# The output projection's block products: weight sums formed in DRAM ahead of time, operand sums stored raw, and a hand-written order

## The chip, the cores and the metric

One Trainium2 chip, one of its cores. The metric is the device time of one launch in microseconds. The kernel before was run three times: 2400.41, 2401.74 and 2396.83 us, median 2400.41. A separate profiled launch took 2404.39 us, of which 2402.6 us lie between its first and its last instruction; the trace and all its views are of that launch.

## What is computed

One layer of a streaming encoder, on 512 prompt frames and 32 frames of a running stream, 544 columns together, with a model width of 2048. The part that matters here:

```python
h = layer_norm(x, ln_in_g, ln_in_b)
proj = h @ w_in                       # 2048 -> 4928
o_h = hgrn2(...)                      # 8 heads of 128, gated, normalised
o_a = mla_attention(...)              # 8 heads of 128
mix = concat([o_h, o_a]) @ w_out      # 2048 -> 2048: the output projection
h1  = layer_norm(ALPHA * h + mix, ln1_g, ln1_b)
ff  = conv_ffn(h1)                    # 2048 -> 5632 -> 2048
y   = layer_norm(ALPHA * h1 + ff, ln2_g, ln2_b)
```

All data are float32. A product in that precision is made of three passes over rounded parts: a value x is split into h = round(x) and l = x - h, and w*a becomes wh*ah + wh*al + wl*ah.

## The kernel before

Features lie on the 128 partitions and the 544 frames along the free axis, in two halves of 272 (`NI`). One matmul multiplies a 128x128 weight tile by 128x272 activations. Weights arrive as 128x1024 float32 tiles of 512 KB (`raw`). ScalarE rounds each to `wh` and VectorE subtracts to get `wl`.

**Stages.** First come the input norm and projections, then attention (`proj_pair` and `attend`, woven together up to about 300 us), then the heads of the recurrence (about 300 to 727 us): for each head h, `divided_qf` and `divided_ig` multiply on TensorE, while `levels(h)` and `finish(h)` of the heads before are stepped in between. After that comes the output projection (about 727 to 963 us), then the feed-forward network to the end.

**Seven products for eight.** Where a product is "divided", a 2x2 block product of weights and activations is done as seven block products (11, s1, s2, s4, s3, 12, 22), with sums of weight blocks and sums of activation blocks as operands. The heads' input products, the feed-forward ones, and groups 1 to 4 of the output projection are of this kind. One such block product is 8 x 3 = 24 matmuls into one PSUM bank.

**Where the sums come from, for the output projection.** The activation sums s1, s2, s3, s4 are made in `finish(h)`. Its tail, in 18 steps, forms each sum with VectorE in `ab`, rounds it with ScalarE (`high`, L988), subtracts with VectorE (`low`, L991), and stores the pair by one DMA from tile `hl`, which has two buffers, to `ou_dr` (L992, `ous` in the trace). The tail therefore needs four ScalarE copies, four VectorE subtractions and four stores per head. The weight sums are made in place while the products run: `Blocks.plus` (L1257) adds two raw tiles on VectorE, and `plus_dma` (L1260) adds another block from DRAM by an accumulating DMA on GpSimd's queue.

**The output projection itself.** `out_first` multiplies group 0 (tiles 0 and 1 of 16) with 192 matmuls, both halves, while the last head's `finish` is stepped. The residual h0 is then loaded into `za` and `zb` (`zt[k]`, L1401; k < 8 on GpSimd's queue, the others on SyncE's), the stored sums into `su` (L1407, GpSimd's queue). `Norm.first` for each half adds tiles 0 and 1 (L1124), gets the column mean through TensorE (L1113, L1118) and centres both. Groups 5 and 6 follow, first half only, with `gemm_half`, 96 matmuls each. All this is ordered by the planner of the tile framework, which places an instruction of a part without a written order as soon as its engine and its inputs are free by its own reckoning.

A block with a written order (`tc.manual_schedule`) then plays groups 1 to 4. The list `oitems` has 11 and 12 of each group first (8 products), then s1, s2, s4, s3, 22 of each group (20 products). `play` does for item n: the sink of item n-1 (`out_sink`, L1734 or L1737, VectorE adds the PSUM bank into `zt`), the matmuls (L1704), the preparation of the weights of item n+2 (L1246, L1247) and the forming for item n+3 (L1257). Products 11, s2, s3 and 22 of a group share one bank; 12, s1 and s4 use the other kind. The sinks of s4 and 22 also call `close_rows` (L1725), which centres two tiles and adds them and their squares to the norm's sums (GpSimd, ScalarE, L1154). The second halves of eight `cH`/`cL` tiles hold s3 during this time; GpSimd puts it there (`place_s3`, L1774), after L1062 has saved the original, and SyncE brings that back at the end (`place_a21`, L1779). Group 7 and the second halves of groups 5 and 6 follow (913 to 963 us).

Of the kernel before, what the change touches and what calls it, by code (L numbers as in the profile page):

```python
# [15 lines left out]
P = 128  # L16
D = 2048
KD = D // P
# [41 lines left out]
def tile_encoder_step(ctx, tc, xp, xs, w_in, w_in4, w_kr, w_q_b, w_kv_b, w_out, w_out4, w_up, w_gate, w_down, w_down2,  # L60
# [17 lines left out]
    ou_dr = {n: [dram.tile([P, 2, 4, NI], F32, name=f"ou{n}{i}", tag=f"ou{n}{i}") for i in range(2)]  # L78
             for n in ("s1", "s2", "s3", "s4")}
    a21_dr = [dram.tile([P, 2, NI], F32, name=f"a21d{k}", tag=f"a21d{k}") for k in range(HK)]  # L80
# [93 lines left out]
    def weave(fills, chains, ratio):  # L174
        chain = (s for g in chains for s in g)
        credit = 0.0
        for g in fills:
            for _ in g:
                credit += ratio
# [201 lines left out]
    with tc.tile_pool(name="mp", bufs=1) as mp, tc.tile_pool(name="psa", bufs=4, space=PSUM) as psa:  # L381
# [273 lines left out]
        run(proj_pair(0))  # L655
        weave([proj_pair(1)], [attend(0)], 2.0)
        weave([proj_pair(2)], [attend(1)], 2.0)
        weave([proj_pair(3)], [attend(2)], 2.0)
        weave([head_ig(0)], [attend(3)], 2.0)
# [15 lines left out]
    with tc.tile_pool(name="gp", bufs=1) as gp, tc.tile_pool(name="psg", bufs=1, space=PSUM) as psg:  # L675
# [60 lines left out]
        class Divided:  # L736
# [174 lines left out]
        def finish(h):  # L911
# [4 lines left out]
            dma(ab[:, 1], d3_dr[h // 2][:, h % 2])  # L916
            vT = gp.tile([P, 5, P], F32, name="vT", tag="vT", bufs=1)
# [66 lines left out]
            hl = {}  # L984

            def high(name, x):
                hl[name] = gp.tile([P, 2, NI], R, name="hl", tag="hl", bufs=2)
                A.activation(hl[name][:, 0], x, AF.Copy)  # L988

            def low(name, x):  # L990
                V.tensor_tensor(out=hl[name][:, 1], in0=x, in1=hl[name][:, 0].bitcast(F32), op=ALU.subtract)  # L991
                dma(ou_dr[name][h // 4][:, :, h % 4], hl[name].bitcast(F32))  # L992
# [6 lines left out]
            high("s1", ab[:, 0])  # L999
            opposite(ab[:, 1], ab[:, 1], o[:, NI:])  # L1000
            yield
            low("s1", ab[:, 0])
            high("s2", ab[:, 1])
            yield
            low("s2", ab[:, 1])
            opposite(ab[:, 1], ab[:, 1], o[:, :NI])
            high("s4", ab[:, 1])
            yield
            low("s4", ab[:, 1])
# [18 lines left out]
        with tc.manual_schedule(engines=MANUAL):  # L1028
# [7 lines left out]
            beside_from(0, finish(1), range(18))  # L1036
            for h in range(2, HEADS):
                s0 = 28 * (h - 2) + 15
                beside_from(s0, levels(h), (0, 2, 4, 6, 8, 10, 12, 13, 14) if h < HEADS - 1 else (0, 1, 3, 4, 6, 8, 9, 11, 12))
                if h < HEADS - 1:  # L1040
                    beside_from(s0 + 15, finish(h), range(18))
# [358 lines left out]
    for k in range(KD):  # L1400
        (G.dma_start if k < HK else dma)(zt[k], h0_dr[k])  # L1401
# [3 lines left out]
    for n in ("s1", "s2", "s4"):  # L1405
        for i in range(2):
            G.dma_start(su[n][i].bitcast(F32), ou_dr[n][i])  # L1407
# [40 lines left out]
    for t in range(2):  # L1448
        for j in range(2):
            z = zt[t][:, H_[j]]  # L1450
            V.scalar_tensor_tensor(out=z, in0=z, scalar=ALPHA, in1=wo_tiles[t][:, PS_[j]], op0=ALU.mult, op1=ALU.add)
            if t:
                run(nrm[j].first(zt[0], zt[1], acc_tile()))
    ko = [CAT_ORDER[4 * kk] // 4 for kk in range(4)]
    for g in (5, 6):
# [1092 lines left out]
```

## Time and profile before

| what | us |
|---|---|
| median of 3 runs | 2400.41 (2396.83 to 2401.74) |
| the profiled launch | 2404.39 |
| its span, first to last instruction | 2402.6 |
| TensorE busy in the span | 2314.2 |
| VectorE busy | 1725.3 |
| ScalarE busy | 1095.3 |
| GpSimd busy | 272.7 |
| moved by DMA | 471.15 MB |

TensorE is busy 96% of the span. A matmul's own duration in the profile (287 ns for 272 columns) is a latency; started one behind the other they follow at about 125 ns, so a count of matmuls gives the time that a stage needs. In a view of waits a row reads "who waited, for whom: us in total, times, longest". In the chain of work that ended last, a row is start, duration, what. In a timeline, a bracket at the end of a row is the idle time of that engine before it and what ended it.

### The profile page before, as it was taken

How to read it: one execution, taken by the hardware profiler on the slowest of the kernel's cores; microseconds unless marked ns; L12 is line 12 of the kernel's file. 1: busy time of each engine (PE TensorE's matmuls, PEld its weight loads, DVE VectorE, ACT ScalarE, POOL GpSimd, SP SyncE). 2: the span in 40 equal slices, each digit the busy share in tenths (PEclk: the TensorE clock that was granted, in tenths of full speed). 3: DMA queues.
4: the chain of work that ended last, by engine and by line, in shares of the span. 5: the costliest groups of instructions: out<-in, count | busy, mean ns of one | idle time of the engine just before them, and what ended most of it. 6: DMA issues, size and time to landing. Idle time of an engine off the chain costs nothing.

```text
span 2402.6 us, 44712 instructions
## 1 busy us (share of the span) xinstructions
PE 2314.2 (96%) x18244; PEld 2294.8 (96%) x18244; DVE 1725.3 (72%) x2413; ACT 1095.3 (46%) x1696; POOL 272.7 (11%) x351
## 2 busy tenths in 40 slices
PE   7999999999997989999999999999999999999997
PEld 7999999999996989999999999999999999999996
DVE  7455587767765577888777777777777777777776
ACT  5345434433443335665555555555555433333323
POOL 1011001000013121010100000010000111111102
PEclk9999999999998999999999999999999999999998
DMA  6332266555568555778676766767676998889832
GB/s 240 102 102 78 81 201 182 140 137 137 137 192 318 179 132 174 237 183 249 170 228 172 211 196 184 220 169 229 173 207 199 352 330 286 264 283 307 286 102 77
DMA packets 177949, 471.15 MB, mean 196 GB/s; under 512 B 16464, under 2 KB 85840, under 8 KB 169808
## 3 DMA queue, kind: packets, MB, share of 16 engines
q1 hardware_dynamic: 144464, 317.95, 38.6%
q0 software_dynamic: 33280, 150.36, 26.5%
q8 instruction: 143, 2.34, 0.4%
q14 instruction: 62, 0.51, 0.1%
HBM read 383.16 MB, written 82.36 MB: 194 GB/s over the span
## 4 chain that ended last, share of the span: by engine, by line
PE 86%; DVE 5%; DMA 4%; ACT 3%; issue 2%; SPq 0%; POOL 0%; ACTq 0%; DVEq 0%; POOLq 0%
PE main L1305 21%; PE acc L1305 16%; PE main L129 10%; PE main L1336 10%; PE main L821 7%; PE acc L1336 7%; PE acc L129 3%; DMA ous<-hl 2%; PE main L1704 2%; PE acc L1704 1%; PE s L886 1%; DMA zb<-h0d 1%; DVE wl L765 1%; PE main L572 1%; PE at L633 1%
## 5 line engine op out<-in xcount | busy, mean ns | idle before, releaser
L1247 DVE TENSOR_TENSOR wl<-raw,wh 128x1024 fp32r<-128x1024 f32 x373 | 456.0, 1223 | 200.7 <-ACT wh L1246 200.5
L1246 ACT ACTIVATE wh<-raw 128x1024 fp32r<-128x1024 f32 x373 | 393.8, 1059 | 407.8 <-PE main L1305 99.0
L1305 PE MATMUL main<-op,wh 128*128 128x272 f32 x1408 | 265.4, 287 | 0.0
L1305 PE MATMUL acc<-ops,wh 128*128 128x272 f32 x1344 | 254.1, 287 | 0.0
L1305 PE MATMUL main<-ops,wh 128*128 128x272 f32 x1344 | 254.1, 287 | 0.0
L1305 PEld LDWEIGHTS main<-op,wh 128*128 128x128 f32 x1408 | 221.0, 188 | 0.0
L1305 PEld LDWEIGHTS acc<-ops,wh 128*128 128x128 f32 x1344 | 211.1, 188 | 0.0
L1305 PEld LDWEIGHTS main<-ops,wh 128*128 128x128 f32 x1344 | 211.0, 188 | 0.0
L1305 PE MATMUL main<-op,wl 128*128 128x272 f32 x704 | 202.9, 288 | 0.3 <-DVE wl L1247 0.3
L1305 PE MATMUL main<-ops,wl 128*128 128x272 f32 x672 | 193.7, 288 | 0.0
L1305 PE MATMUL acc<-ops,wl 128*128 128x272 f32 x672 | 193.7, 288 | 0.0
L1305 PE MATMUL acc<-op,wh 128*128 128x272 f32 x832 | 157.5, 288 | 1.0 <-ACT ea L1556 1.0
L1246 ACT ACTIVATE wh<-rawl 128x1024 fp32r<-128x1024 f32 x93 | 98.9, 1063 | 116.9 <-PE acc L1305 43.8
L129 PE MATMUL main<-aH,wh 128*128 128x272 f32 (+2 forms) x608 | 150.7, 299 | 0.4 <-ACT wh L297 0.2
L129 PE MATMUL main<-aH,wl 128*128 128x272 f32 (+2 forms) x608 | 148.3, 295 | 2.7 <-DVE wl L298 1.8
L129 PE MATMUL main<-aL,wh 128*128 128x272 f32 (+2 forms) x608 | 148.1, 295 | 1.0 <-DVE aL L286 1.0
L765 DVE TENSOR_TENSOR wl<-raw,wh 128x1024 fp32r<-128x1024 f32 x84 | 102.8, 1224 | 59.6 <-ACT wh L760 58.6
L1305 PEld LDWEIGHTS main<-op,wl 128*128 128x128 f32 x704 | 132.2, 188 | 0.5 <-DVE wl L1247 0.5
L1247 DVE TENSOR_TENSOR wl<-rawl,wh 128x1024 fp32r<-128x1024 f32 x93 | 113.7, 1223 | 26.2 <-ACT wh L1246 26.1
L1305 PEld LDWEIGHTS acc<-op,wh 128*128 128x128 f32 x832 | 130.4, 188 | 1.2 <-ACT ea L1556 1.2
L821 PE MATMUL main<-s,wh 128*128 128x272 f32 x576 | 118.5, 303 | 9.6 <-ACT hproj L806 9.6
L1305 PEld LDWEIGHTS main<-ops,wl 128*128 128x128 f32 x672 | 126.2, 188 | 0.0
(491 smaller groups left out, 6133.7 us busy)
## 6 DMA issues: line engine op xcount, KB each, us to landing
raw<-in_w_in SPq DMA_DIRECT2D x76, 512.0 KB, 4.2
raw<-in_w_up SPq DMA_DIRECT2D x71, 512.0 KB, 5.5
raw<-in_w_gate SPq DMA_DIRECT2D x71, 512.0 KB, 4.7
raw<-in_w_down SPq DMA_DIRECT2D x67, 512.0 KB, 9.1
opd<-ohl SPq DMA_DIRECT2D x20, 1088.0 KB, 5.5
ops<-opd POOLq DMA_DIRECT2D x20, 1088.0 KB, 11.6
raw<-in_w_out SPq DMA_DIRECT2D x36, 512.0 KB, 4.5
raw<-in_w_up POOLq DMA_DIRECT2D x35, 512.0 KB, 5.3
```

What stands on the lines that cost most here:

```text
L129: PE.matmul(ps, ww[:, wcols[0]:wcols[1]], aa[:, hs[j]], start=first and i == 0, stop=last and i == 2, skip_group_check=True)
L572: PE.matmul(ps[:, j * 512:j * 512 + 256], l[k][:, a:b], r4(w[:, k:k + 1, :])[:, 0, :, 128:256], start=k == 0 and i == 0, stop=k == 1 and i ...
L633: PE.matmul(po[:, :P], vt[:, k, j, :], t[:, k * P:(k + 1) * P], start=k == 0, stop=k == b)
L765: V.tensor_tensor(out=wl, in0=self.t(self.key), in1=wh.bitcast(F32), op=ALU.subtract)
L821: PE.matmul(out, ww[:, k * P:(k + 1) * P], aa, start=name in ("11", "s1", "12") and k == 0 and q == 0, stop=k == HK - 1 and q == 2, skip_g ...
L886: PE.matmul(ps[:, j * 64:(j + 1) * 64], Kp[:, a:b], Qv[:, j * bt:(j + 1) * bt, 1, :], start=True, stop=True)
L1246: A.activation(wh, src, AF.Copy)
L1247: V.tensor_tensor(out=wl, in0=src, in1=wh.bitcast(F32), op=ALU.subtract)
L1305: PE.matmul(ps, ww[:, k * P:(k + 1) * P], aa, start=self.first and k == 0 and i == 0, stop=k == n - 1 and i == 2, skip_group_check=True)
L1336: PE.matmul(banks[:, 512 * u:512 * u + NI], ww[:, (u * n + k) * P:(u * n + k + 1) * P], aa, start=self.first and k == 0 and i == 0, stop=k ...
L1704: PE.matmul(self.bank, ww[:, k * P:(k + 1) * P], aa, start=self.first and k == 0 and i == 0, stop=k == HK - 1 and i == 2, skip_group_check ...
```

## The change

1. **Weight sums in DRAM.** For each of the groups 1 to 4, four tiles of 512 KB in DRAM (`wf_dr`: s1, s2, s3, 22) are filled by GpSimd's DMA queue, DRAM to DRAM: 32 transfers, 16 plain copies and 16 accumulating ones, in six phases that depend on each other (`forming`). Twenty are written into the program of the attention stage (one in every seven steps, the rest at its end), and twelve into the heads, one beside each s2 product. Each product of the projection then loads one finished weight block with SyncE; `Blocks.plus` and `plus_dma` are no longer used here.
2. **Operand sums raw.** The tail of `finish` makes three sums (s1, s2, s4) with three VectorE instructions and stores them unsplit with one DMA from tile `sm`; 15 steps in place of 18. They are loaded by half as many bytes (six loads of 544 KB) and split by ScalarE and VectorE beside the first products (`split_su`). s3 needs no store of its own: the difference that attention already stored is loaded by SyncE (`load_21`) and split (`split_21`), and the original is loaded and split again afterwards (`restore`).
3. **Order by hand.** The start of the projection after `out_first`, with groups 5 and 6, is one block with a written order: the matmuls of a quarter of a group (`step`, 24 matmuls) stand between the steps of `Norm.first`, and the loads stand in a given order on the queues of GpSimd and SyncE.
4. **A product between each sink and its bank.** The four 11 products come first, then s1, s2, s4, s3, 12, 22 of each group, so 12 stands between the sink of s3 and the product 22 that adds to the same bank. `close_rows` is called after 12 and 22, as fill work that `drain` places where room is left.

```diff
+    sm_dr = [dram.tile([P, 3, 4, NI], F32, name=f"sm{i}", tag=f"sm{i}") for i in range(2)]
+    wf_dr = {(g, n): dram.tile([P, HK * P], F32, name=f"wf{g}{n}", tag=f"wf{g}{n}")
+             for g in range(1, 5) for n in ("s1", "s2", "s3", "22")}
...
+    def forming(phase):
+        for g in range(1, 5):
+            f = {n: wf_dr[g, n] for n in ("s1", "s2", "s3", "22")}
+            for out, src, add in ((("s1", "11", False), ("s3", "12", False)), (("s1", "12", True), ("s3", "22", True)),
+                                  (("s2", "s1", False),), (("s2", "22", True),), (("22", "s2", False),), (("22", "21", True),))[phase]:
+                src = f[src] if src in f and not add else out_block(g, src)
+                yield lambda out=f[out], src=src, add=add: G.dma_start(out, src, **({"accum_op": ALU.add, "max_dma_last_dim": 2048} if add else {}))
...
+        def tick():
+            ticks[0] += 1
+            if ticks[0] % 7 == 0:
+                form_next(12)
+
+        weave([proj_pair(0)], [], 0.0, tick)
...
+        while len(forms) > 12:
+            form_next()
...
                 if self.name == "s2":
                     G.dma_start(self.t("11"), self.src("21"), accum_op=ALU.add)
+                    form_next()
...
-            minus(ab[:, 0], o[:, NI:], ab[:, 0])
-            high("s3", ab[:, 1])
-            yield
-            low("s3", ab[:, 1])
...
+            minus(sm[:, 0], o[:, NI:], ab[:, 0])
+            opposite(sm[:, 1], ab[:, 1], o[:, NI:])
+            yield
+            opposite(sm[:, 2], sm[:, 1], o[:, :NI])
+            dma(sm_dr[h // 4][:, :, h % 4], sm)
...
-                    if k >= HK:
-                        for n, t in enumerate((cH[k], cL[k])):
-                            G.dma_start(a21_dr[k - HK][:, n], t[:, NI:].bitcast(F32))
...
+        for _ in range(3):
+            raw_next()
+        for k in (0, 1, 2, 4, 6):
+            G.dma_start(zt[k], h0_dr[k])
+        for k in (10, 11, 12, 13, 8):
+            dma(zt[k], h0_dr[k])
+        for k in (3, 5, 7):
+            G.dma_start(zt[k], h0_dr[k])
+        for n in ("s1", "s2"):
+            for i in range(2):
+                load_su(n, i)
+        split_next()
+        split_next()
...
+        step(five, ws56[0], 0, 0)
+        split_next()
+        next_firsts()
+        step(five, ws56[1], 0, 1)
+        split_next()
+        next_firsts()
...
-            if name in ("s4", "22"):
-                close_rows(g, 0 if name == "s4" else 1)
-            return 0.4
+            if name in ("12", "22"):
+                fill(0.75, lambda: close_rows(g, 0 if name == "12" else 1))
+                breaks()
+            return 0.44
...
+        oitems = [out_item(g, "11", X[g]) for g in range(1, 5)]
         for g in range(1, 5):
...
+            oitems += [out_item(g, name, {"12": BC[0], "s1": BC[1], "s4": BC[1]}.get(name, X[g]))
+                       for name in ("s1", "s2", "s4", "s3", "12", "22")]
...
+        def restore():
             for k in range(HK):
+                load_21(k, cat_dr[4 + k // 2][:, k % 2, NI:])
...
+        ohooks = {0: [lambda: split_su("s1", 1)], 1: [lambda: split_su("s2", 0)], 2: [lambda: split_su("s2", 1)],
+                  3: [lambda: split_su("s4", 0)], 4: [lambda: split_su("s4", 1)], 5: [lambda: split_21(range(4))],
+                  6: [lambda: split_21(range(4, 8))],
```

More of the change, by code (lines that the diff above doesn't have):

```diff
@@ L1034, in beside_from @@
                     turns.setdefault(slot + n, []).append(gen)
-            beside_from(0, finish(1), range(18))
+            beside_from(0, finish(1), range(15))
             for h in range(2, HEADS):
@@ L1446, in post, with step @@
             o[0] += 1
-    for t in range(2):
-        for j in range(2):
[L1450 to L1455, printed above, removed]
-        ws = [out_piece(kk, g) for kk in ko]
-        for t in range(2):
-            shifted(2 * g + t, 0)
-        ps = pair_half(acc_tile(), 0)
-        gemm_half(ps, ws, cact, CAT_ORDER, 0)
-        for t in range(2):
-            joined(2 * g + t, 0, ps[t], G)
+    def step(outs, w, j, kk):
+        for t in range(2):
+            for k in range(4):
+                kg = CAT_ORDER[4 * kk + k]
+                mm3([(outs[t], j)], (w[0][:, kg % 4], w[1][:, kg % 4]), (t * P, t * P + P), cact(kg),
+                    kk == 0 and k == 0, kk == 3 and k == 3)
@@ new lines, in tile_encoder_step, with raw_next, split_next, next_firsts @@
+    ko = [CAT_ORDER[4 * kk] // 4 for kk in range(4)]
+    early = [psA.tile([P, 1024], F32, name="acc", tag="acc") for _ in range(2)]
+    with tc.manual_schedule():
+        order56 = [(kk, g) for g in (5, 6) for kk in ko]
+        raws56, ws56 = [], []
+        def raw_next():
+            if len(raws56) < 8:
+                kk, g = order56[len(raws56)]
+                raws56.append(load_raw(w_out[kk, g - 4], 4, 256))
+        def split_next():
+            ws56.append(split_w(raws56[len(ws56)], 4, 256))
+            raw_next()
+        for _ in range(3):
+            raw_next()
+        for k in (0, 1, 2, 4, 6):
[9 more added lines that the diff above has]
+        split_next()
+        firsts = []
+        for j in range(2):
+            for t in range(2):
+                z = zt[t][:, H_[j]]
+                V.scalar_tensor_tensor(out=z, in0=z, scalar=ALPHA, in1=wo_tiles[t][:, PS_[j]], op0=ALU.mult, op1=ALU.add)
+            firsts.append(nrm[j].first(zt[0], zt[1], early[0][:, 512 * j:512 * j + 512]))
+            next(firsts[j])
+        def next_firsts():
+            for f in firsts:
+                next(f, None)
+        five, six = pair_half(early[1], 0), pair_half(main_tile(), 0)
+        step(five, ws56[0], 0, 0)
[4 more added lines that the diff above has]
+        next_firsts()
+        for i in range(2):
+            load_su("s4", i)
+        step(five, ws56[2], 0, 2)
+        next_firsts()
+        split_next()
+        shifted(10, 0)
+        shifted(11, 0)
+        step(five, ws56[3], 0, 3)
+        split_next()
+        for k in range(HK):
+            load_21(k, d3_dr[k // 2][:, k % 2])
+        step(six, ws56[4], 0, 0)
+        split_next()
+        for t in range(2):
+            joined(10 + t, 0, five[t], G)
+        step(six, ws56[5], 0, 1)
+        split_next()
+        shifted(12, 0)
+        shifted(13, 0)
@@ L1688, in tile_encoder_step, with form, prep, cost @@
     NU = 0
-    class Out(Item):
+    class Product(Item):
+        def form(self):
+            return 0.0
+        def prep(self):
+            self.w = rounded(self.g.raw["w"].t, HK)
+            release(self.g, "w")
+            return self.cost(2)
+        def cost(self, ahead):
+            return HK * 0.149 + 0.06 if ahead == 2 else 0.0
         def operand(self, k):
@@ L1791, in tile_encoder_step @@
             split_seventh(n)
+        while fills:
+            drain(3.0)
     ou_stack.close()
@@ L1798, in tile_encoder_step @@
             x1_op[name] = [op_tile(name, i) for i in range(2)]
-        def step(outs, w, j, kk):
-            for t in range(2):
-                for k in range(4):
-                    kg = CAT_ORDER[4 * kk + k]
-                    mm3([(outs[t], j)], (w[0][:, kg % 4], w[1][:, kg % 4]), (t * P, t * P + P), cact(kg),
-                        kk == 0 and k == 0, kk == 3 and k == 3)
         sr = [None] * 2
```

114 lines of the change are left out of this document (53 added, 61 removed).

## The prediction

> **What bounds the kernel now.** I read the page's head first, then busy time by stage, then who TensorE waits for, and for each long wait the chain behind it.
>
> ```profile
> span 2402.6 us, 44712 instructions
> core 0: us, PE busy (x) PEld busy (x) DVE busy (x) ACT busy (x) POOL busy (x), PEclk, DMA share, GB/s
> 400.00:727.00 327.00, 311.17 (x2487) 308.71 (x2486) 229.11 (x411) 134.83 (x214) 30.23 (x37) 0.97 0.55 152
> 727.00:755.30 28.30, 28.30 (x233) 28.30 (x233) 20.83 (x35) 10.16 (x16) 16.34 (x29) 1.00 0.93 316
> 755.30:812.00 56.70, 34.39 (x222) 33.43 (x221) 19.45 (x32) 11.91 (x18) 7.13 (x10) 0.76 0.72 272
> 812.00:913.00 101.00, 89.73 (x680) 88.54 (x679) 69.61 (x89) 32.84 (x43) 20.17 (x24) 0.97 0.58 149
> 913.00:963.00 50.00, 50.00 (x403) 50.00 (x403) 38.98 (x54) 28.34 (x42) 5.79 (x7) 1.00 0.50 164
> PE main L821 <- ACT hproj L806: 9.6, 4, 3.4
> PE s L886 <- DVE Kp L892: 6.2, 4, 4.2
> PE acc L1113 <- DVE n_e L1124: 13.7, 1, 13.7
> PE main L1704 <- DVE za L1734: 9.7, 3, 3.3
> PE main L1113 <- DVE n_e L1124: 8.0, 1, 8.0
> ```
>
> The first column pair is the stage and its length. TensorE bounds the kernel, so only its idle time and its slow time can be gained. It is idle 15.8 us of the heads (400 to 727), 22.3 us at the start of the projection (755.3 to 812) and 11.3 us in the block products (812 to 913). The other stages that the change touches, 727 to 755 and 913 to 963, have none.
>
> **Heads.** What stands behind the first two waits:
>
> ```profile
>   DMA ous<-hl: 57.3, 9
> 526.63 0.43 ACT L988 ACTIVATE hl<-ab 128x272 fp32r<-128x272 f32 x1 [9.74 <-DMA ous<-hl]
> 519.00 7.53 DMA ous<-hl
> 528.34 4.80 PE main L821 x24
> 587.37 4.55 PE main L821 x24
> 708.76 5.11 PE main L821 x24
> 857.18 3.01 PE acc L1704 x24
> ```
>
> The view of tile hl gives 57.3 us in nine waits of ScalarE for a store of the split sums to land, since hl has only two buffers. ScalarE works in order, so the next wh, behind it VectorE's wl and the bank copy L806 are late; TensorE runs dry. After a wait 24 matmuls take 4.80, 4.55 and 5.11 us where an undisturbed 24 take 3.01. That is 1.8 + 1.5 + 2.1 = 5.4 us at three places. With the 15.8 us idle, the heads lose 21 us.
>
> **Start of the projection.**
>
> ```profile
> 753.68 7.17 DMA ous<-hl
> 765.16 21.98 DMA zb<-h0d
> 799.79 12.16 PE acc L129 x96
> zb<-h0d SPq DMA_DIRECT2D x8, 272.0 KB, 17.8
> us<-ous POOLq DMA_DIRECT2D x6, 1088.0 KB, 13.0
> ```
>
> The last head's store delays ScalarE once more, then the loads of zb queue behind that store on SyncE and share the DMA engines with six 1088 KB loads of the split sums. VectorE, in order, stands at zb while TensorE waits for n_e, which is next in VectorE's order. Work there: two groups of 96 matmuls at 12.16 us are 24.3 us, and four small mean steps some 2.5 us; the window has 56.7 us. **Lost: 30 us**, 22.3 of it idle and the rest at the granted clock of 0.76.
>
> **Block products.** VectorE before the first late 22:
>
> ```profile
> 846.15 0.44 DVE L1734 TENSOR_TENSOR za<-za,acc 128x272 f32<-128x272 f32 x1 [0.32 <-PE acc L1704]
> 846.62 0.73 DVE L1725 TENSOR_TENSOR za<-za,n_cb 128x544 f32<-128x544 f32 x1
> 847.85 1.66 DVE L1154 TENSOR_TENSOR n_s<-n_s,n_e 128x272 f32<-128x272 f32 x2 [0.50 <-ACT n_e L1150]
> 849.43 1.21 DVE L1247 TENSOR_TENSOR wl<-raw,wh 128x1024 fp32r<-128x1024 f32 x1
> 850.68 1.22 DVE L1257 TENSOR_TENSOR raw<-raw,raw 128x1024 f32<-128x1024 f32 x1
> 851.82 0.43 DVE L1734 TENSOR_TENSOR za<-za,main 128x272 f32<-128x272 f32 x1
> 852.39 4.78 PE main L1704 x24
> 872.43 4.77 PE main L1704 x24
> 892.44 3.25 PE main L1704 x24
> ```
>
> Product 22 needs the bank of s3, whose sink (851.82) is queued behind the closing of rows, a split and a forming. This happens in three groups. 672 matmuls at 3.01 us per 24 are 84.3 us, and 6 of group 7 are 0.8, so of 101.0 us **16 are lost**.
>
> [...]
>
> **The change, part by part.**
>
> *Tail of finish.* Per head it removes four ScalarE copies of 0.43 us, four VectorE subtractions of about as much (the L1734 row, same shape), and four stores through a two-buffer tile; it adds one store which nothing waits for before the next head, some 58 us later (the slow blocks of two heads, 528.34 and 587.37, lie 59 us apart). ScalarE then has no DMA in its path. Of the 21 us I take 19: ScalarE's chain of wl, forming and wh is next in line and could leave a fraction of a microsecond per head. The bounds are 12 and 24 (further slow matmuls that I have not quoted).
>
> *Start of the projection.* When out_first ends, TensorE goes straight on with 24 matmuls (3.0 us) of group 5, whose weights are split beforehand; VectorE has in that time four scalings and two additions at 0.44 us, 2.6 us. So the mean step finds its operand, and so on at each quarter. VectorE's work in the stage is 10 splits of 1.21, some 20 pieces of 0.44, four of 0.8 and one wide split of about 1.3, together 25.4 us against 27 us of TensorE: just covered. The cover that can fail is the DMA. From 727 until the products begin, 8 weight loads and the first 5 of the products (512 KB), 16 of h0 (272 KB), six sums (544 KB) and 8 tiles of 136 KB must come: 15360 KB, 15.7 million bytes. At the 316 GB/s of the window from 727 to 755 that is 50 us, and there are about 55. The stores and loads of the saved halves (L1062, L1774) that filled this window go away. The loads stand in order of need, but h0 on SyncE stands ahead of the fourth weight load. I leave 5 us of stall: **25 gained**. Bounds: 30, and 12 if nearly all loads start only at 755 (14 million bytes at 316 GB/s are 44 us).
>
> *Block products.* The number of 512 KB transfers per group stays at seven (five loads and two accumulations before, seven loads after). VectorE loses eight formings of 1.22 us, so they can't be late any more. Between the sink of s3 and 22 stands product 12, 3.0 us in which the sink has to pass, at worst, one split (1.21), and closing pieces that drain places by room. In the first seven products VectorE has sink 0.44, split 1.21 and 1.3 (`split_su`, 1088 wide, from the 1.21 of 1024) or 1.45 (eight pieces split in two hooks, four at 0.36 to 0.44): 2.95 to 3.3 us of 3.0, with a lead of two products. I leave 2 us: **14 gained**, bounds 8 and 16.
>
> *Splitting the originals again* (`restore`): 8 VectorE pieces of about 0.4 us and 8 of ScalarE, in 913 to 963, where VectorE is busy 39 of 50 us and ScalarE 28. Covered: 0; without cover 3.2.
>
> *Forming in DRAM.* The trace has no DRAM-to-DRAM transfer. The nearest rows:
>
> ```profile
> q0 software_dynamic: 33280, 150.36, 26.5%
> raw<-in_w_in POOLq DMA_DIRECT2D x6, 512.0 KB, 5.3
> 10.58 0.15 DVE L348 TENSOR_TENSOR lbt<-par 128x8 f32<-128x8 f32 x1
> DMA  0689999999999999999960000346896235335028
> 37.92 1.18 POOL L261 TENSOR_SCALAR rs<-mv 128x1 f32<-128x1 f32 x1 [5.28 <-DVE mv L260]
> ```
>
> By the first, GpSimd's queue takes 0.265 x 2402.6 / 150.36 = 4.2 us of all 16 engines per MB, 2.2 us per form, 71 us for 32. Where the DMA engines have room (attention, heads) this costs nothing. Where they are full it delays what they carry. I take a ninth of it, **8 us**; bounds 0 and 45 (below, first rival). A gain is excluded: no other work becomes shorter by it.
>
> **Sum:** 19 + 25 + 14 - 8 = 50 us. Against the profiled launch's 2404.4 that is 2354.4. The median of the runs shown lies 4.0 us under that launch, so I forecast **2350 us**.
>
> **Rivals.**
>
> *A: the forms run ahead to the start.* Only their own order binds them; they wait for no tile of the kernel. The planner does issue free instructions far ahead: L348 stands behind the whole first projection in the program and ran at 10.58 us. The row of tenths is the DMA engines' busy share from 0 to 60 us in 40 slices: full from about 4 to 30 us, with x and the first weights. The forms would take half of the engines there, and 26 us of loads would become up to 52. With 26 lost and the other 58 gained, 32 remain: 2368 us, with 2355 to 2390 around it. Against it: each form holds GpSimd's queue, and the later phases need the earlier to land. Chance 0.20.
>
> *B: the start of the projection stays bound by DMA.* If h0 and the sums can't start before their memory is free at 755, 12 gained in place of 25: 2363 us. For it: 0.93 DMA share from 727 to 755. Against: some of that traffic goes. Chance 0.12.
>
> *C: slower, by GpSimd's queue.* It works in order. A form that waits for an earlier one to land stops all behind it, the rs steps of the input norm (the last at 37.92) among them, and normalising, in order on VectorE, stops TensorE. At 5.3 us to land, 32 forms one after the other are 170 us; 170 - 38 = 132 us lost, net 132 - 58 = 74 slower: 2474. It decides from about (58 + 38) / 5.3 = 18 forms ahead of the last rs step. Against: phases have 4 or 8 independent forms, which overlap. Chance 0.08. [...]
>
> *D: the waits come back elsewhere.* With hl gone, VectorE's forming chain (busy 229 of 327 us in the heads) or the splits in the first seven products become late: 15 to 20 gained, 2383. Chance 0.05.
>
> **How the numbers follow.** Forecast 0.55, A 0.20, B 0.12, C 0.08, D 0.05. The forecast's own range is 2335 (24 + 30 + 16 - 0 = 70 at most, less what seldom comes together) to 2362. A and D reach to 2390, where I cut. Low is 2334. About 0.2% (5 us) is what a measurement of this kernel can tell from no change. Faster by more: 0.55 + 0.12 + 0.05 and nearly all of A, 0.87. Within: 0.04. Slower: 0.09.
>
> **What would show it.** Right: no ScalarE wait on a store in the heads, granted clock 1.00 there; TensorE's first block product at 768 to 776 us (812 less 19 and 25, with up to 8 for the forms); no wait of L1704 matmuls on their sink; 28 products in 86 us. Wrong: matmuls that start well after 28 us, or DVE waiting for rs (A or C); TensorE waiting for wl in groups 5 and 6 (B); sinks late by split_su (D). The forecast would be wrong above all if the forms land in a stretch where DMA or GpSimd's order is needed.

## The result and the profile after

| | median us | runs, lowest to highest |
|---|---|---|
| before | 2400.41 | 5, 2396.83 to 2401.74 |
| changed | 2411.51 | 5, 2410.58 to 2414.03 |

The ratio is 1.0051, with a 95% interval of 1.0036 to 1.0065: the changed kernel is slower by half a per cent (11 us by the medians, 8 between the spans of the two profiled launches), where the prediction had it faster by two.

The head of the page of the changed kernel, with TensorE's busy tenths, its granted clock and the DMA engines' share in 40 slices of 60 us each:

```profile
span 2410.8 us, 44619 instructions
PE   2499999999999999999999999999999999999997
PEclk8699999999999999999999999999999999999998
DMA  9753226555556854668677677767677998889832
```

The same row of TensorE before:

```profile
PE   7999999999997989999999999999999999999997
```

TensorE is two and four tenths busy in the first two slices and full from there on; before, it was seven and nine tenths busy in them and weaker only at two places in the output projection (721 to 781 and 841 to 901 us). To see how much each stage took I cut both executions at the same four events: the first and the last matmul of the heads' main product, and of the output projection's block products. The rows are those of the view of one source line (count, shortest/median/longest in ns, first and last start in us). Before:

```profile
L821 PE MATMUL main<-aH,wh x384: 283/288/393, 367.5 to 726.3; 128*128 128x272 f32 x192
L1704 PE MATMUL main<-aH,wh x96: 283/288/428, 811.8 to 912.5; 128*128 128x272 f32 x96
```

After:

```profile
L850 PE MATMUL main<-aH,wh x384: 282/288/397, 438.2 to 771.6; 128*128 128x272 f32 x192
L1792 PE MATMUL main<-aH,wh x96: 283/288/428, 830.2 to 920.3; 128*128 128x272 f32 x96
```

| stage | before | after | difference |
|---|---|---|---|
| up to the first matmul of the heads | 367.5 | 438.2 | +70.7 |
| heads | 358.8 | 333.4 | -25.4 |
| from the heads to the first block product | 85.5 | 58.6 | -26.9 |
| block products | 100.7 | 90.1 | -10.6 |
| from there to the end of the span | 1490.1 | 1490.5 | +0.4 |

The three stages that the change was about gain 62.9 us, where the prediction had 58. All of it is given back, and 8 us more, in a stretch that the change was not about: the first 120 us. What TensorE waits for longest there, and VectorE behind it:

```profile
PE tp L297 <- DVE x L287: 39.6, 3, 22.1
PE main L146 <- DVE aL L305: 36.5, 2, 34.6
DVE x L287 <- POOL rs L281: 57.5, 4, 35.4
```

In the kernel before, the view of tile rs has for the same wait:

```profile
  DVE x L268: 1.8, 2
```

L287 is the normalising of x, which needs the rs step that GpSimd makes at L280 and L281 (L261 and L262 before). GpSimd's timeline shows what stands around these steps:

```profile
24.85 0.60 POOL L281 TENSOR_TENSOR rs<-rs,nhalf 128x1 f32<-128x1 f32 x1
25.39 0.73 POOL L91 DMA_DIRECT2D wf4s<-in_w_out  x1
26.12 1.01 POOL L91 DMA_DIRECT2D wf1s<-in_w_out  x1
37.67 0.92 POOL L91 DMA_DIRECT2D wf1s<-in_w_out  x1 [10.54 <-issue]
46.24 0.88 POOL L91 DMA_DIRECT2D wf2s<-in_w_out  x1 [7.64 <-issue]
...
64.28 0.89 POOL L91 DMA_DIRECT2D wf3s<-in_w_out  x1 [4.88 <-issue]
64.87 0.59 POOL L280 TENSOR_SCALAR rs<-mv 32x1 f32<-32x1 f32 x1
69.80 0.95 POOL L91 DMA_DIRECT2D wf4s<-in_w_out  x1 [4.34 <-issue]
70.43 0.93 POOL L281 TENSOR_TENSOR rs<-rs,nhalf 32x1 f32<-32x1 f32 x1
...
109.36 0.59 POOL L280 TENSOR_SCALAR rs<-mv 128x1 f32<-128x1 f32 x1
109.54 0.92 POOL L91 DMA_DIRECT2D wf<-wf1s  x1
110.14 0.93 POOL L281 TENSOR_TENSOR rs<-rs,nhalf 128x1 f32<-128x1 f32 x1
```

L91 is a forming transfer. All 32 ran ahead of the work that they were written beside, the last of them at 139.18 us; 24 stand on GpSimd's queue ahead of the last rs pair. Most of the accumulating ones go out only after 4.3 to 10.5 us of idle time, though the eight of one phase need nothing of each other, and the bracket names no releaser ("issue"). So the rs steps between them come late, the last at 110.1 us where it was at 39.2 before: 70.9 us, the same as the shift of all that follows.

### The profile page after: what moved, and what is told of

It is laid out like the page before. It is cut to its first block, busy times and chain, and to the rows that moved or that the text cites. A ratio compares the mean times of both kernels' runs of the same rounds, so it can differ in the third digit from the quotient of the medians.

```text
span 2410.8 us, 44619 instructions
## 1 busy us (share of the span) xinstructions
PE 2301.5 (95%) x18244; PEld 2284.0 (95%) x18244; DVE 1716.4 (71%) x2395; ACT 1096.8 (45%) x1686; POOL 272.6 (11%) x343
## 4 chain that ended last, share of the span: by engine, by line
PE 89%; issue 4%; DMA 2%; DVE 2%; ACT 2%; POOL 1%; SPq 0%; ACTq 0%; DVEq 0%; POOLq 0%
PE main L1312 21%; PE acc L1312 16%; PE main L850 10%; PE main L1343 10%; PE main L146 10%; PE acc L1343 7%; PE acc L146 3%; PE main L1792 2%; PE s L915 2%; PE acc L1792 2%; PE main L591 1%; PE at L652 1%; PE at L621 1%; DMA raw<-in_w_in 1%; DMA wf1s<-wf1s 0%
## 5 line engine op out<-in xcount | busy, mean ns | idle before, releaser
L146 PEld LDWEIGHTS main<-aL,wh 128*128 128x128 f32 x608 | 106.1, 194 | 37.2 <-DVE aL L305 37.1
L1254 DVE TENSOR_TENSOR wl<-rawl,wh 128x1024 fp32r<-128x1024 f32 x93 | 113.8, 1223 | 25.6 <-ACT wh L1253 25.4
L793 DVE TENSOR_TENSOR wl<-raw,wh 128x1024 fp32r<-128x1024 f32 x84 | 103.1, 1227 | 35.9 <-ACT wh L788 35.0
```

Of the source, the lines that this page charges most:

```text
L146: PE.matmul(ps, ww[:, wcols[0]:wcols[1]], aa[:, hs[j]], start=first and i == 0, stop=last and i == 2, skip_group_check=True)
L1254: V.tensor_tensor(out=wl, in0=src, in1=wh.bitcast(F32), op=ALU.subtract)
```

## The experiments

Two theories of the lost start stand against each other. **C**, a rival of the prediction: the forms block GpSimd's in-order queue, and the rs steps behind them are late. **A**, another: the forms' bytes crowd the DMA engines while x and the first weights come in (in the changed kernel a load of x takes 12.7 us to land in the median, 7.6 before). Two explanations of the odd spacing came up later: **R**, the forms wait for room in the memory that the kernel sets aside with `dynamic_dma_scratch_size=1024` ("descriptors" in the expectations is the author's word for what it holds, which no view shows), and **S**, accumulations follow one another whatever their size. Times are medians; each ratio is against the kernel before, run on the same chip (2398.6 to 2399.9 us).

### All forms held in their places

```diff
     def form_next(n=0):
         if len(forms) > n:
-            forms.pop(0)()
+            with tc.issue_after(behind[0]):
+                forms.pop(0)()
...
+            behind[0] = G.tensor_tensor(out=x, in0=x, in1=cos, op=ALU.mult).ins
```

and likewise for the other GpSimd instructions that a form follows in the program. An order on the queue is all that this adds; no wait comes with it.

> Every forming transfer is held on GpSimd's queue behind the GpSimd instruction that stands just before it in the program (a rope step, attend's subtraction, the heads' own accumulation), so none can run ahead to the first 140 us. Theory C (the accumulating transfers were drawn to the start, went out one at a time on GpSimd's in-order queue, 79.0 us of idle there, and the rs steps of the norm stood behind them: VectorE waited 57.5 us for rs) and theory A (the forms' bytes drew DMA from x and the first weights at the start: some 12 us late) both expect the start as before (first memset of ql near 79 us, not 148.8) and 2411 - 70 = about 2342 us, up to 2355 if a form that is now in a later phase makes a GpSimd step there late. A third theory, that something else of the change costs the time, expects about 2400 or more.

Measured: 2387.5 us, ratio 0.9956 (0.9941 to 0.9972). The start is as before (the last rs step at 39.3 us), but only 24 us come back. TensorE's longest wait, and GpSimd's queue at that time:

```profile
PE s L918 <- DVE attnT L934: 28.4, 1, 28.4
```

```profile
299.86 0.93 POOL L91 DMA_DIRECT2D wf1s<-in_w_out  x1
309.50 0.91 POOL L91 DMA_DIRECT2D wf1s<-in_w_out  x1 [8.71 <-issue]
...
350.80 0.90 POOL L91 DMA_DIRECT2D wf4s<-in_w_out  x1 [4.94 <-issue]
...
353.31 1.40 POOL L711 MEMSET attnT<- 128x544 f32 x2
```

The same thing at another place. After attention the program issues at once what is left of the twenty (`while len(forms) > 12`). Twelve in a row take 53 us ahead of two fills of `attnT`, and the heads wait for those. With the slow matmuls around that wait (granted clock 0.75 from 300 to 360 us) the heads begin at 408.1 us, 39 later than in the run without forms below. The expectation allowed 13 us for such a step and missed that a whole row of forms would stand there.

### Held behind the norm only

```diff
-                G.tensor_tensor(out=rs[:n, 1:2], in0=rs[:n, 0:1], in1=nhalf[:n, 0:1], op=ALU.pow)
+                behind[0] = G.tensor_tensor(out=rs[:n, 1:2], in0=rs[:n, 0:1], in1=nhalf[:n, 0:1], op=ALU.pow).ins
```

with the same `form_next`, and no other anchor.

> Only one condition is added: no forming transfer before the last rs step of the norm; from there on they may run as early as before, one after another (32 accumulating and copying transfers, some 5 to 8 us each, about 140 us). If C is all (only the rs steps stood behind them), this is as good as the run with every form held: about 2342 us. If GpSimd's queue blocks later work too (rope's and attend's GpSimd steps at 80 to 220 us), or the DMA traffic itself disturbs the weights of the first projections, it lies between: 2350 to 2390 us, with TensorE waits in that stretch.

Measured: 2400.1 us, ratio 1.0002 (0.9983 to 1.0021). One row of TensorE's timeline has it (start, duration, operation, idle time before it and what ended it):

```profile
142.86 2.08 PE L453 MATMUL at<-ident,r 128*128 128x128 f32 x8 [54.17 <-POOL r L448]
```

The forms now start at 39.8 us and the next step of GpSimd that matters, the `pow` of the query norm, comes out behind 29 of them, 10 us beyond the range that I gave. Each time the place differs and the mechanism is the same: whichever small GpSimd step lies behind the run of forms takes the loss.

### No forms at all

```diff
-    forms = [f for phase in range(6) for f in forming(phase)]
+    forms = []
...
-            src = wf_dr[g, name] if (g, name) in wf_dr else out_block(g, {"11": "11", "12": "21", "s4": "22"}[name])
+            src = out_block(g, {"11": "11", "12": "21", "s4": "22", "s1": "11", "s2": "12", "s3": "22", "22": "21"}[name])
```

> Leaves out the forming of the weight sums: the four products that use sums take the plain blocks of the output weight straight from DRAM instead, so bytes read by the products are the same. All theories under which the forms cost the 70 us expect about 2340 us (2411.5 less 70, and up to 5 less for the forms' traffic elsewhere). If the rest of the change is what costs, it stays at 2400 or more. Set against the run with all forms held, the difference is the price of the forms themselves, which the prediction took as 8 us.

Measured: 2343.6 us, ratio 0.9778 (0.9747 to 0.9809). So the forms cost the changed kernel 2411.5 - 2343.6 = 67.9 us, and everything else in the change is worth 56 us against the kernel before on the same chip, 2 less than the sum of its three terms. (This run leaves out the weight sums, so it gives a price and not a usable kernel.) The cuts of this run:

```profile
L850 PE MATMUL main<-aH,wh x384: 282/288/397, 368.8 to 702.1; 128*128 128x272 f32 x192
L1792 PE MATMUL main<-aH,wh x96: 283/288/432, 760.3 to 850.5; 128*128 128x272 f32 x96
```

Heads 333.3, on to the first product 58.2, products 90.2 us: the same as in the changed kernel, within half a microsecond. What the forms cost is lost before the heads.

### The bytes alone

With the weights of the products as in the run before:

```diff
-    forms = [f for phase in range(6) for f in forming(phase)]
+    wc_dr = [dram.tile([P, HK * P], F32, name=f"wc{i}", tag=f"wc{i}") for i in range(32)]
+    forms = [lambda i=i: G.dma_start(wc_dr[i], out_block(1 + i % 4, ("11", "12", "22", "21")[i // 4 % 4])) for i in range(32)]
```

> The 32 forming transfers become 32 plain copies of 512 KB from DRAM to DRAM, each to a place of its own, so none waits for another, and they may run ahead to the start as before; the sums themselves are left out (the products take the plain blocks). 32 x 1.05 MB moved (read and written) stay, the waits on GpSimd's queue go. Theory A (bytes): it loses at the start about as much as the changed kernel or more, 2400 us or above. Theory C (accumulations one at a time on the in-order queue): the rs steps are not blocked by waits, only transfers crowd x and the first weights: 33.6 MB at the 289 GB/s seen there are 116 us of traffic that x, par and w_in share, so a loss of 10 to 40 us on 2340: 2350 to 2380 us.

Measured: 2379.5 us, ratio 0.9931 (0.9905 to 0.9958), at the upper end of what C allowed. 32 copies, all ahead of the heads, cost 35.9 us over the run without. No copy waits long on GpSimd (0.3 us in all); VectorE waits for rs 2.7 us in all; but x lands late (12.4 us in the median, against 7.6 before), and GpSimd's rs steps wait longer for the statistics of the norm (45.4 us, 31.7 without forms). So A is real, and half as large as the whole loss.

### The queue alone

To leave the queue and take the bytes, the forms were cut down to 16 of 1024 columns, an accumulating one still in 256 pieces, and the products again take the plain blocks:

```diff
-                yield lambda out=f[out], src=src, add=add: G.dma_start(out, src, **({"accum_op": ALU.add, "max_dma_last_dim": 2048} if add else {}))
+                yield lambda out=f[out], src=src, add=add: G.dma_start(out[:, :16], src[:, :16], **({"accum_op": ALU.add, "max_dma_last_dim": 32} if add else {}))
```

> The changed kernel with forms of 16 of 1024 columns, an accumulating one still cut into 256 pieces (of 32 bytes), so that the descriptors stay and nearly all bytes go; the products take the plain blocks (the weight sums are left out). Theory R (descriptors' room) gives each accumulating form that follows another a wait of its landing, now without crowding: some 2.5 to 5 us instead of 4.3 to 10.5, so that the last rs step comes at about 60 to 90 us instead of 110, and the whole takes 2360 to 2390 us. If the bytes were all that counted, it equals the run without forms, 2343 to 2347 us.

Measured: 2396.0 us, ratio 0.9990 (0.9975 to 1.0004), outside both ranges: 52.4 us over the run without forms, with 0.26 MB on GpSimd's queue up to 120 us. The rs steps (first and last start) and who waits for them:

```profile
L281 POOL TENSOR_TENSOR rs<-rs,nhalf x5: 566/598/1071, 28.0 to 91.0; 128x1 f32<-128x1 f32 x4, 32x1 f32<-32x1 f32 x1
  DVE x L287: 48.9, 3
```

The last rs step is 51.5 us later than without forms (39.5), which is nearly the whole loss. A form lands in 2.9 us here and the gaps are shorter, as expected. What I had wrong is the order: shorter transfers let the planner put all 32 ahead of the third rs pair, where the changed kernel has 24 ahead of the fifth. C needs no bytes.

C and A are not two shares of one sum (52.4 + 35.9 is more than 67.9): in the changed kernel both delay the same norm, and crowding lengthens each landing for which the queue waits (7.3 us in the median there, 2.9 with few bytes).

### Why accumulations stand apart

Two numbers of the changed kernel were altered, one in each of two runs: the pieces of an accumulation, and the size given as `dynamic_dma_scratch_size`.

```diff
-"max_dma_last_dim": 2048
+"max_dma_last_dim": 8192
```

> The changed kernel with one number altered: an accumulating form is cut into pieces of 8192 bytes instead of 2048 (64 pieces for 512 KB instead of 256; the bytes, the order and the number of transfers stay). In the changed kernel an accumulating form went out 4.3 to 10.5 us after the one before, with nothing to wait for, while plain copies of 48 packets went out every 0.5 us. Theory R (the space that the kernel sets aside for the descriptors of GpSimd's transfers, 1024 bytes, holds those of one cut-up accumulation and little more, so the next one waits on GpSimd until the first has gone): with a quarter of the pieces several fit, the idle time of 79.0 us before the forms falls below 25, the rs steps come at most some 10 us late by the queue, and what is left is the crowding of the DMA engines, 2350 to 2385 us. Theory S (accumulations follow one another whatever their size): the gaps stay at 4 us or more and the time at 2405 to 2415 us.

```diff
-    nc = bacc.Bacc("TRN2", target_bir_lowering=False, num_devices=1, dynamic_dma_scratch_size=1024)
+    nc = bacc.Bacc("TRN2", target_bir_lowering=False, num_devices=1, dynamic_dma_scratch_size=2048)
```

> The changed kernel with one number altered: 2048 bytes instead of 1024 set aside for the descriptors of GpSimd's transfers; the forms are as in the changed kernel. Theory R: room for two or three cut-up accumulations at once, so the gaps between them shrink (idle before the forms 79.0 us down to 20 to 50) and the time lies between 2365 and 2400 us. Theory S: gaps and time unchanged, 2405 to 2415 us.

Measured: with fewer pieces 2390.3 us, ratio 0.9963 (0.9950 to 0.9976), 5 us over R's range; with more room 2381.2 us, ratio 0.9918 (0.9901 to 0.9935). Neither is S's 2405 to 2415. GpSimd's timeline from the first accumulation on, with fewer pieces:

```profile
27.49 1.71 POOL L91 DMA_DIRECT2D wf1s<-in_w_out  x2
28.55 2.25 POOL L91 DMA_DIRECT2D wf2s<-in_w_out  x2
29.56 3.12 POOL L91 DMA_DIRECT2D wf3s<-in_w_out  x2
```

and with more room:

```profile
26.01 1.94 POOL L91 DMA_DIRECT2D wf1s<-in_w_out  x2
27.21 1.65 POOL L91 DMA_DIRECT2D wf2s<-in_w_out  x1
37.51 0.89 POOL L91 DMA_DIRECT2D wf2s<-in_w_out  x1 [8.66 <-issue]
```

Where one accumulation went out and the next waited 10.54 us, six now start within 3 us in the one run, and three go out before a wait in the other. Idle time with no releaser before the forms is none and 30.3 us in place of 79.0. S falls; R holds. That the 256 pieces by themselves take GpSimd the time of the gap falls too: with more room and as many pieces three go out in a row. What remains is in part A: in the run with fewer pieces TensorE waits longest for the sample rows of x themselves (23.5 us). But VectorE also still waits 14.6 us (fewer pieces) and 22.1 us (more room) for rs, behind forms that wait for earlier ones to land or for room. No run separates the two shares.

The five runs with the forms at the start, beside the one without:

| forms | idle by "issue", us | last rs step | heads begin | time |
|---|---|---|---|---|
| none | - | 39.5 | 368.8 | 2343.6 |
| plain copies | - | 67.2 | 406.6 | 2379.5 |
| more room | 30.3 | 74.6 | 405.8 | 2381.2 |
| fewer pieces | none | 70.3 | 416.7 | 2390.3 |
| few bytes | 41.6 | 91.0 | 419.4 | 2396.0 |
| as changed | 79.0 | 110.1 | 438.2 | 2411.5 |

### Forms one or two at a time

The fault is then where the forms stand, not that there are any. On the kernel with all forms held, the number left for the heads goes from 12 to 24, and a second place is added in each double head:

```diff
-                form_next(12)
+                form_next(24)
...
-        while len(forms) > 12:
+        while len(forms) > 24:
...
                 if name == "s1":
-                    G.dma_start(self.t("12"), self.src("22"), accum_op=ALU.add)
+                    behind[0] = G.dma_start(self.t("12"), self.src("22"), accum_op=ALU.add).ins
+                    form_next()
```

> The forms are spread further: the eight first copies, which hold nothing up, stay beside attention, and the other 24 go out in the twelve double heads, two in each, each held behind one of the two accumulations that the head issues on GpSimd anyway; TensorE ran full there with one form per head in the run with all forms held. That run lost 28.4 us at 300 to 353, where twelve forms in a row stood on GpSimd's queue ahead of two fills of attnT. If the forms' price is only what stands behind them on that queue, this gives 2345 to 2352 us (the run without forms, 2343.6, and a little). If their bytes cost time wherever they lie, or a form now makes the head's own accumulation late, it stays at 2360 to 2390 with TensorE waits on wh or wl in the heads.

Measured: 2347.1 us, ratio 0.9782 (0.9768 to 0.9797). The heads from 400 to 680 us, in the columns of the view of busy time by stage:

```profile
400.00:680.00 280.00, 279.83 (x2300) 278.56 (x2300) 201.83 (x348) 112.79 (x167) 41.08 (x47) 1.00 0.69 175
```

TensorE is full there with the forms running. Then all 32 went into the heads:

```diff
-                form_next(24)
+                form_next(32)
...
-        while len(forms) > 24:
+        while len(forms) > 32:
...
                     behind[0] = G.dma_start(self.t("11"), self.src("21"), accum_op=ALU.add).ins
                     form_next()
+                    if len(forms) > 16:
+                        form_next()
```

> As the run with the forms spread over attention and heads, but the eight first copies too wait for the heads (two more of them behind one of the two accumulations in the first heads), so that attention carries none. If the 3.4 us between that run and the run without forms come from the copies in attention, this gives 2343 to 2346 us; if they come from GpSimd or DMA in the heads, it gives 2347 to 2352 us.

Measured: 2344.8 us, ratio 0.9770 (0.9755 to 0.9784). The bound of 16 leaves three forms over at the end, so this run leaves out the last three accumulations of block 22. With a bound of 8 none is left:

> All 32 forms in the heads, as in the run before this one, but with a third form in each of the first eight double heads, so that none is left over (that run left out the last three accumulations of block 22). By that run's 2344.8 us and three forms more behind accumulations that have room, 2344 to 2348 us, the same as or up to 3 us below the run that spread them over attention and heads (2347.1). If a third form behind one accumulation makes GpSimd's next step late, as twelve in a row did at 300 to 353 us, it comes out at 2350 us or more, with TensorE waits in the heads.

Measured: 2345.1 us, ratio 0.9785 (0.9766 to 0.9805), 2.2% below the kernel before and 2.8% below the changed one. It has the lowest median of the versions that compute everything, but the run with two places cannot be told from it: its ratio is 0.9782, and its median lies 2 us above on another chip. Its row of the same view, from the first to the last matmul of the heads:

```profile
368.50:701.80 333.30, 332.38 (x2730) 330.71 (x2728) 240.84 (x419) 138.62 (x207) 51.06 (x60) 1.00 0.75 196
```

Against the run without forms this is 1.5 us, less than its own runs spread (2343.1 to 2349.1): so placed, 32 forms cost next to nothing, although GpSimd still stands 34.8 us before them. Nothing that stands behind them there is late for TensorE.

### The order of the products alone

On the kernel without forms (which leaves out the weight sums), 12 and 22 change places:

```diff
-                       for name in ("s1", "s2", "s4", "s3", "12", "22")]
+                       for name in ("s1", "s2", "s4", "s3", "22", "12")]
```

> The run without forms (which leaves out the weight sums), and product 12 put behind 22 instead of between s3 and 22, so that 22 needs the bank of s3 at once, as before the change. The prediction's term for the block products was 14 us, bounds 8 to 16. If the order alone brings it, this is 8 to 16 us above the run without forms: 2352 to 2360 us. If the rest (eight formings of 1.22 us less on VectorE) is what brought it, the sink of s3 is passed in time and the loss is four times the sink and its latency, about 1 us each: 2345 to 2348 us.

Measured: 2347.3 us, ratio 0.9783 (0.9769 to 0.9798), that is 3.6 us above the run without forms. TensorE's waits for a sink:

```profile
PE main L1792 <- DVE za L1820: 1.8, 3, 0.6
PE main L1792 <- DVE zb L1820: 1.5, 1, 1.5
```

Four waits of 0.6 to 1.5 us, where before three of about 3.2 us stood, two of them with slow matmuls behind (the next 24 take 4.78, 4.77 and 3.25 us; undisturbed 3.01). By the medians the product in between is worth 3.6 us, but the intervals of the two ratios overlap; in the traces the block products take 95.6 us from first to last matmul (759.7 to 855.3) and 90.5 without the swap (760.3 to 850.8), so 5 us there. That is less than half of what the stage gained. The rest would go with the formings that no longer stand ahead of the sink on VectorE; no run shows this by itself.

### The stores of the split sums

The kernel before, with one edit in `finish`:

```diff
-                dma(ou_dr[name][h // 4][:, :, h % 4], hl[name].bitcast(F32))
+                dma(ou_dr[name][h // 4][:, :, h % 4], aH[0].bitcast(F32).rearrange("p (a x) -> p a x", a=2))
```

> The kernel before with one edit in the heads: the four stores of the split sums keep their place and their bytes, but take them from an operand tile that is never rewritten in the heads, so that no copy of ScalarE waits for a store to land (the split sums in DRAM are then not the real ones). The ScalarE and VectorE work of the splits stays. If the wait for the two buffers of hl is what cost the heads 25.5 us (their matmuls take 359.1 us from first to last before and 333.6 in the changed kernel), the heads take 334 to 339 us and the whole 2374 to 2381 us. If the four copies and subtractions themselves, or the traffic of the stores, take part, the heads stay at 345 us or more.

Measured: 2357.4 us, ratio 0.9824 (0.9808 to 0.9840), well below the range: 42 us from one line. From this run's views of the heads' product, of the stores and of the DMA issues (the last number there is the median from issue to landing):

```profile
L821 PE MATMUL main<-aH,wh x384: 282/288/397, 366.4 to 700.4; 128*128 128x272 f32 x192
L1704 PE MATMUL main<-aH,wh x96: 283/288/444, 763.9 to 866.1; 128*128 128x272 f32 x96
L992 SPq DMA_DIRECT2D ous<-aH x32: 512/526/1577, 46.6 to 388.7; - x32
zb<-h0d SPq DMA_DIRECT2D x8, 272.0 KB, 6.7
```

The heads take 334.0 us, 24.8 of the 25.4 that the change gained there, with the four copies and subtractions still in place. ScalarE's 57.3 us of waits for a store are gone. So the copies and subtractions cost next to nothing, and the stores cost nearly all of it. The run doesn't quite do what I wrote: the stores did not keep their place. Their source was ready early, and the planner moved them to 46.6 to 388.7 us. Wait and most of the stores' traffic left the heads together. That traffic of this size need not cost anything there is seen in the run with all forms in the heads, where 32 forms of 512 KB ran beside the heads and these took 333.3 us; so the wait is what is left to blame.

The stage up to the first product also falls, from 85.5 to 63.5 us. The loads of zb no longer queue on SyncE behind a store that waits for its data: they land in 6.7 us, not 17.8. Of the 26.9 us that the change gained at the start of the projection, 22 come with this alone. The smaller loads and the hand-written order can have added 5 to it; what they would bring with the stores as they were is not tested.

## Why the prediction was wrong

**Heads: right in mechanism, low in size.** 19 us stood in the sum, with 24 as the upper bound; 25.4 came. The mechanism is shown by the run with the other source. Idle time was sized well: from the first to the last matmul of the heads TensorE sat idle 16.9 us before and 0.9 after (332.77 of 333.70 us busy, granted clock 1.00), where the sum had 15.8 to gain. Slow matmuls were worth 9.5 us (342.24 us busy before), where I had counted 5.4 at three places. The 2 us that I took off for the next delay in ScalarE's chain did not come.

**Start of the projection: right in sum** (25, measured 26.9), by luck in part: what brought it was less the new order than the store that no longer blocks SyncE. The first product starts at 760.3 us without forms, 8 us ahead of the window that I named. Rival B does not appear.

**Block products: a size off.** 14 us, measured 10.6. I expected 28 products in 86 us; from the first matmul to the last they take 90.3. The waits before 22 are gone as forecast (9.7 us before), but the sink still holds TensorE up at a new place, among the first four products:

```profile
835.09 1.28 DVE L1417 TENSOR_TENSOR us<-us 128x1088 fp32r<-128x1088 f32 x1
836.30 0.43 DVE L1823 SCALAR_TENSOR_TENSOR za<-za,main 128x272 f32<-128x272 f32 x1
836.87 0.36 PE L1792 MATMUL main<-aH,wh 128*128 128x272 f32 x1 [3.45 <-ACT us L1416]
844.70 0.44 DVE L1823 SCALAR_TENSOR_TENSOR za<-za,main 128x272 f32<-128x272 f32 x1 [0.29 <-PE main L1792]
845.28 0.36 PE L1792 MATMUL main<-aH,wh 128*128 128x272 f32 x1 [0.62 <-DVE za L1823]
```

The bracket puts the long wait down to ScalarE's split of a sum, which ended last (836.86), 0.01 us ahead of the matmul. The second product does not use that sum. The sink of the first product ended at 836.73, 0.14 us ahead, the distance that also stands between sink and matmul at 845.28. The first two 11 products share one PSUM tile, the other two the next, and both waits stand before the second user of a tile. So most likely both are waits for a sink; the first is late on VectorE behind the split of a sum, which is rival D's sign ("sinks late by split_su") in one place. No run tests it. About 1.5 us of slow matmuls follow it (24 take 4.53 us from 836.87 on, with a granted clock of 0.64 up to 841.5). The lead of two products that my sum relied on did not exist there.

The three terms add up to 58 and the stages to 62.9; that these lie close is partly luck, since the heads gave 6.4 more and the block products 3.4 less.

**Restore: right**, nothing to be seen (+0.4 us to the end).

**Forming in DRAM: the step that failed.** The sum had 8 us, "a ninth" of 71 us of DMA time, with bounds of 0 and 45; it cost 67.9. I priced a transfer by the DMA engines' time and took for granted that the 32 would run where they were written, in attention and heads. They ran at once. The text had seen the row that says so (L348 at 10.58 us) and still gave A and C 0.28 together. As separate cases they were wrong too: they came together. Against C I wrote that "phases have 4 or 8 independent forms, which overlap". The accumulating ones did not: most of them went out only after 4.3 to 10.5 us of idle time, for want of room in `dynamic_dma_scratch_size` (79.0 us of idle time at 1024, 30.3 at 2048), of which none of the rows that I read speaks. C's own bound, 18 forms ahead of the last rs step, was passed (there were 24), but its reckoning of 5.3 us for each form was met by luck: twelve of the 24 were copies, which went out without such a wait, and most of the other twelve held the queue for 5.5 to 11.6 us each. One smaller slip: the chance of 0.87 for a faster kernel holds only 0.15 of A's 0.20, not "nearly all".

In the changed kernel's trace a form's wait for an earlier one stands on the queue that issues it, as C has it: GpSimd stands 12.2 us before forms until earlier ones have landed (9.1 the longest). The 79.0 us by "issue" are a wait of another kind on the same queue. VectorE waits 57.5 us for the rs steps behind them.

## What to carry to other kernels

A transfer that depends on nothing is placed by the planner, not by its line: give it an anchor on its queue, and ask what is the next urgent instruction behind it there. Transfers issued from an engine that also computes can cost by that engine's order as much as by their bytes (here 52.4 us with hardly any bytes, 35.9 us with the bytes and hardly any wait); put them a few at a time where nothing urgent follows, as here in the heads, where 32 of them cost about 1.5 us, which is within the noise. When several parts are summed, measure the kernel at the same events before and after: the ledger showed at once that three parts had come true and that a fourth stage had paid.

## What the runs showed of the hardware

In this kernel the size given as `dynamic_dma_scratch_size` and the number of pieces decide how closely GpSimd's accumulations follow one another. Before the forms GpSimd stands idle by "issue" for 79.0 us at 1024 with 256 pieces, for 30.3 us at 2048 with 256 pieces, and not at all at 1024 with 64 pieces. From the first accumulation on, one goes out and the next waits 10.54 us; at 2048 three go out and the fourth waits 8.66 us; with 64 pieces six go out without such a wait (27.49 to 32.68 us; one issue takes up to 2.6 us there, about 0.9 in the changed kernel). With forms of few bytes, seven copies of 8 KB went out in a row and the eighth waited:

```profile
2.48 1.31 POOL L91 DMA_DIRECT2D wf1s<-in_w_out  x2
3.78 1.04 POOL L91 DMA_DIRECT2D wf2s<-in_w_out  x2
4.81 1.03 POOL L91 DMA_DIRECT2D wf3s<-in_w_out  x2
5.84 0.52 POOL L91 DMA_DIRECT2D wf4s<-in_w_out  x1
7.99 0.53 POOL L91 DMA_DIRECT2D wf4s<-in_w_out  x1 [1.63 <-issue]
```

From 40 to 64 us in the changed kernel GpSimd's queue moved 1088 packets and 2.10 MB, which is four accumulations of 256 pieces at 272 packets each. How much of that size one transfer takes up, no run shows.

In the changed kernel a compute step of GpSimd behind a waiting transfer is late by that wait, even if it needs nothing from it: of the pair of rs steps at 64.87 and 70.43 us, the second comes out behind a form that went out after 4.34 us of idle time. Plain copies, of 32 packets each (192 packets and 3.15 MB for six of them, up to 26.1 us in the changed kernel; the 48 in an expectation above was a misreading), pass about 0.5 us apart in the run of plain copies, seven of them in 3.62 us.
